# A rotation by 90 degrees: the first store held back until all loads but the last megabyte have landed

## The chip, the cores and the metric

The kernel runs on one core of a Trainium2 chip. The metric is device time in microseconds (us). Before the change the median of three runs is 123.41 us (123.36 to 123.59). Besides these runs there is one profiled execution, whose trace has the start and length of each instruction, each DMA packet and each semaphore update.

## The reference

The input is 32 x 3 images of 256 x 256 float32 (25.17 MB), and each is turned by a quarter:

```python
def setup_inputs():
    batch, c, h, w = 32, 3, 256, 256
    return {"x": np.random.randn(batch, c, h, w).astype(np.float32)}

def reference(x: np.ndarray) -> np.ndarray:
    return np.rot90(x, k=-1, axes=(-2, -1)).astype(np.float32)
```

Nothing is computed: every element is read once, moved, and written once, 50.33 MB in all.

## The kernel before, in words

All the data fits in SBUF at once. The rows of all images are cut into twelve slabs of 2 MB (128 partitions x 16 rows of 256 elements), which are held in five groups of 2, 2, 4, 2 and 2 slabs. A group is one tile (named u for each) with a buffer of its own, so no load ever waits for a buffer.

Loading. SP (SyncE) issues all loads from one queue. Group 0 comes in as two transfers of 1 MB (L55) and one of 2 MB (L56); groups 1 to 4 come in as ten transfers of 2 MB each (L61), two, four, two and two of them. A transfer of a group with I slabs fills every I-th partition, with both halves (index a) of each partition's row; in the last group it is 64 partitions x 2 halves x 16 KB. In all there are thirteen loads.

Turning. DVE transposes 32 x 32 blocks, a quarter of a group's data at a time, and writes the result in reversed order to where it belongs (L69 for group 0; L85 and L90 for the others). A quarter that would overwrite data still needed goes to a spare buffer first (L85, in PSUM or in one extra tile of SBUF), and ACT copies it home later (L75, L95). There are 24 DVE instructions of 3.6 to 4.0 us and 16 ACT copies of 0.5 to 1.9 us.

Storing. The same queue of SP issues twelve stores of 2 MB: two for group 0 (L103), ten for groups 1 to 4 (L108), in the order of the groups. In SP's program all stores stand behind all loads. The first store of each group waits for the group's last DVE instruction and ACT copy.

Two things set the order around the change. First, SP works its program through in order: an instruction that waits holds back everything behind it. Secondly, the framework gives the transfers of this queue eight semaphores in turn, and a transfer that reuses one waits until the transfer that had it before has landed; so at most eight transfers are open at a time. Before the change, the first store (L103) waits for the landing of load 5 (counted from 0) and for DVE and ACT, and is issued at 27.73 us; the second is issued at 32.51 us.

Of the kernel before, what the change touches and what calls it, by code (L numbers as in the profile page):

```python
# [1 line left out]

# [4 lines left out]


@with_exitstack  # L10
def kernel(
    ctx: ExitStack,
    tc: tile.TileContext,
    x: bass.AP,
    out: bass.AP,
):

    nc = tc.nc
    fp32 = mybir.dt.float32

    B, C, H, W = x.shape
    P = nc.NUM_PARTITIONS
    R = 16  # L30
    E = R * W
    hw = R // 2
    low, high = slice(0, hw), slice(hw, R)

    rows_in = x.rearrange("b c h w -> (b c h) w")
    rows_out = out.rearrange("b c h w -> (b c h) w")

    sizes = (2, 2, 4, 2, 2)
    first = [sum(sizes[:n]) for n in range(len(sizes))]
    groups = [  # L40
        ctx.enter_context(tc.tile_pool(name=f"group{n}", bufs=1)).tile([P, s, E], fp32, name=f"u{n}")
        for n, s in enumerate(sizes)
    ]
    psum = ctx.enter_context(tc.tile_pool(name="psum", bufs=1, space=bass.MemoryType.PSUM))
    spare = [psum.tile([P, E // 2], fp32, name=f"spare{h}") for h in range(2)]
    extra = ctx.enter_context(tc.tile_pool(name="extra", bufs=1)).tile([P, E // 2], fp32, name="extra")

    def rows_of(rows, n):
        return rows[first[n] * P * R : (first[n] + sizes[n]) * P * R]


    ld = rows_of(rows_in, 0).rearrange("(s i p r) w -> s i p (r w)", s=2, i=2, p=P)
    home = [groups[0][:, s].rearrange("p (i f) -> p i f", i=2) for s in range(2)]
    for i in range(2):
        nc.sync.dma_start(out=home[0][:, i], in_=ld[1, i])  # L55
    nc.sync.dma_start(out=home[1], in_=ld[0].transpose([1, 0, 2]))  # L56
    for n in range(1, len(sizes)):
        I = sizes[n]
        ld = rows_of(rows_in, n).rearrange("(a i m r) w -> i m a (r w)", a=2, i=I, m=P // I)
        for i in range(I):  # L60
            nc.sync.dma_start(  # L61
                out=groups[n].rearrange("p s f -> p (s f)").rearrange("p (a f) -> p a f", a=2)[i::I],
                in_=ld[i])

    def turn_slab(src, dsts):
        s = src.rearrange("p (i r g c) -> p c r g i", i=2, r=R // 2, c=R)
        for h, d in enumerate(dsts):
            d = d.rearrange("p (c k r) -> p c r k", c=hw, r=R // 2)[:, :, ::-1, ::-1]
            nc.vector.transpose(out=d, in_=s[:, h * hw : (h + 1) * hw])  # L69

    u = groups[0]
    turn_slab(u[:, 0], spare)
    turn_slab(u[:, 1], [u[:, 0, : E // 2], u[:, 0, E // 2 :]])
    for h in range(2):
        nc.scalar.copy(out=u[:, 1, h * E // 2 : (h + 1) * E // 2], in_=spare[h])  # L75

    def turn_group(n, held):
        I = sizes[n]
        T = I // 2
        K = W // (R * T)  # L80
        u = groups[n].rearrange("p s f -> p (s f)")
        src = u.rearrange("p (a t r g c) -> p t c r g a", a=2, t=T, r=R, c=R)
        dst = u.rearrange("p (i c k t r) -> p t c r k i", i=I, c=R, k=K, t=T)[:, ::-1, :, ::-1, ::-1, :]
        for t in range(T):
            nc.vector.transpose(  # L85
                out=held[t].rearrange("p (i c k r) -> p c r k i", i=I, c=hw, k=K)[:, :, ::-1, ::-1, :],
                in_=src[:, t, low, low])
        for c, r in ((low, high), (high, high), (high, low)):
            for t in range(T):
                nc.vector.transpose(out=dst[:, t, c, r], in_=src[:, t, c, r])  # L90
        back = u.rearrange("p (i c k t r) -> p t i c k r", i=I, c=R, k=K, t=T)[:, ::-1]
        for t in range(T):
            kept = held[t].rearrange("p (i c k r) -> p i c k r", i=I, c=hw, k=K)
            for i in range(I):
                nc.scalar.copy(out=back[:, t, i, low, :, high], in_=kept[:, i])  # L95

    for n, held in enumerate(([extra], spare, [spare[0]], [spare[1]]), 1):
        turn_group(n, held)


    st = rows_of(rows_out, 0).rearrange("(s i m r) w -> i m s (r w)", s=2, i=2, m=P // 2)
    for a in range(2):
        nc.sync.dma_start(out=st[a], in_=groups[0][a::2])  # L103
    for n in range(1, len(sizes)):
        st = rows_of(rows_out, n).rearrange("(a i m r) w -> a m i (r w)", a=2, i=sizes[n], m=P // 2)
        for i in range(0, sizes[n], 2):
            for a in range(2):
                nc.sync.dma_start(out=st[a][:, i : i + 2], in_=groups[n][a::2, i : i + 2])  # L108


# [1 line left out]
_INS = ['x']  # L112
_OUTS = [((32, 3, 256, 256), 'float32')]


# [23 lines left out]
```

## Time and profile before

| what | value |
|---|---|
| median of three runs | 123.41 us |
| profiled execution | 123.44 us |
| its span | 121.6 us |
| DVE busy | 87.4 us, 24 instructions |
| ACT busy | 14.9 us, 17 instructions |
| bytes moved | 50.33 MB, half read from HBM, half written |
| mean rate over the span | 414 GB/s |
| first issue of a load / of a store | 0.73 us / 27.73 us |
| last issue of a store | 104.56 us |

Times in the profile count from the start of the span; the profiled execution's own time is 1.84 us above its span. The profile gives the busy time of each engine, the mean share and rate of the sixteen DMA engines in forty equal slices of the span (3.04 us each), groups of instructions by source line, who waited for whom, and for a DMA issue the time from issue to landing. Landing means the update that completes the transfer's semaphore: each of the sixteen DMA engines adds one when its share is done. An issue row is written as start, length of the issue on SP's queue (SPq), line, and the tiles out<-in. In a stretch of time the columns are DVE, ACT and POOL busy time with their instruction counts, the granted clock of TensorE (not used here), the DMA share and GB/s.

### The profile page before, as it was taken

Reading aid. Unit: us, or ns where it says so; the run is one execution under the profiler, and the core shown is the slowest. Engines: PE = TensorE matmul, PEld = TensorE weight load, DVE = VectorE, ACT = ScalarE, POOL = GpSimd, SP = SyncE. Lnnn points to the kernel's source line nnn. Section 1 sums busy time; section 2 is a strip of 40 time slices with the busy share of each in tenths; the row PEclk is TensorE's granted clock in tenths of the full one; section 3 lists DMA queues with packets and bytes.
Section 4 is the critical chain, followed back from the end, with each engine's and each line's share of the span. In section 5 each row is a group of like instructions: output and inputs, shape, how many; then the busy total and the mean of one; then the engine's idle time right before and its main releaser. Section 6 shows DMA issues by size and latency. Waiting matters only on the chain.

```text
span 121.6 us, 130 instructions
## 1 busy us (share of the span) xinstructions
DVE 87.4 (72%) x24; ACT 14.9 (12%) x17; POOL 0.2 (0%) x4
## 2 busy tenths in 40 slices
DVE  0039999999994099999999949999999995000000
ACT  0000400470004100000000354000240004100000
POOL 0000000000000000000000000000000000000000
DMA  4999999998989899999999999999999999999993
GB/s 92 423 426 434 442 431 431 436 506 356 506 356 506 350 431 431 426 431 431 377 409 431 431 431 431 442 431 431 431 431 442 431 436 431 431 431 431 431 431 135
DMA packets 3472, 50.33 MB, mean 414 GB/s; under 512 B 400, under 2 KB 400, under 8 KB 400
## 3 DMA queue, kind: packets, MB, share of 16 engines
q1 hardware_dynamic: 3472, 50.33, 97.7%
HBM read 25.17 MB, written 25.17 MB: 414 GB/s over the span
## 4 chain that ended last, share of the span: by engine, by line
DVE 42%; DMA 30%; issue 7%; SPq 4%; ACT 2%; ACTq 1%; DVEq 0%
DVE u L90 30%; DMA u<-in_x_dram 30%; DVE spare L85 12%; SPq L61 3%; ACT u L95 2%; ACTq L134 1%; SPq L55 1%; SPq L56 0%; DVEq L85 0%
## 5 line engine op out<-in xcount | busy, mean ns | idle before, releaser
L90 DVE STREAM_TRANSPOSE u<-u 128x2048 f32<-128x2048 f32 x15 | 54.7, 3665 | 0.4
L85 DVE STREAM_TRANSPOSE spare<-u 128x2048 f32<-128x2048 f32 x4 | 14.3, 3586 | 5.9 <-DMA u<-in_x_dram 4.3
L95 ACT COPY u<-spare 128x512 f32<-128x512 f32 (+1 forms) x12 | 8.0, 743 | 55.9 <-DVE u L90 55.9
L69 DVE STREAM_TRANSPOSE spare<-u 128x2048 f32<-128x2048 f32 x2 | 7.1, 3584 | 8.1 <-DMA u<-in_x_dram 8.1
L69 DVE STREAM_TRANSPOSE u<-u 128x2048 f32<-128x2048 f32 x2 | 7.8, 3990 | 0.0
L75 ACT COPY u<-spare 128x2048 f32<-128x2048 f32 x2 | 3.6, 1870 | 8.7 <-DVE u L69 8.7
L85 DVE STREAM_TRANSPOSE extra<-u 128x2048 f32<-128x2048 f32 x1 | 3.9, 3899 | 0.0
L95 ACT COPY u<-extra 128x1024 f32<-128x1024 f32 x2 | 2.0, 1043 | 11.3 <-DVE u L90 11.3
L75 ACT ACT_TABLE_LOAD x1 | 1.3, 1283 | 13.1 <-DMA u<-in_x_dram 13.1
L123 POOL MEMSET const-bfloat16-1.0<- 128x1 bf16 x1 | 0.1, 101 | 0.0
L123 POOL MEMSET const-uint8-127<- 128x1 uint8 x1 | 0.1, 101 | 0.0
L123 POOL MEMSET const-float32-0.0<- 128x1 f32 x1 | 0.1, 98 | 0.2 <-issue 0.2
L123 POOL MEMSET const-float32-1.0<- 128x1 f32 x1 | 0.1, 98 | 0.0
## 6 DMA issues: line engine op xcount, KB each, us to landing
out_dram<-u SPq DMA_DIRECT2D x12, 2048.0 KB, 20.6
u<-in_x_dram SPq DMA_DIRECT2D x11, 2048.0 KB, 32.3
u<-in_x_dram SPq DMA_DIRECT2D x2, 1024.0 KB, 5.8
```

Source lines behind the costliest of these rows:

```text
L55: nc.sync.dma_start(out=home[0][:, i], in_=ld[1, i])
L61: nc.sync.dma_start(out=groups[n].rearrange("p s f -> p (s f)").rearrange("p (a f) -> p a f", a=2)[i::I], in_=ld[i])
L69: nc.vector.transpose(out=d, in_=s[:, h * hw : (h + 1) * hw])
L75: nc.scalar.copy(out=u[:, 1, h * E // 2 : (h + 1) * E // 2], in_=spare[h])
L85: nc.vector.transpose(out=held[t].rearrange("p (i c k r) -> p c r k i", i=I, c=hw, k=K)[:, :, ::-1, ::-1, :], in_=src[:, t, low, low])
L90: nc.vector.transpose(out=dst[:, t, c, r], in_=src[:, t, c, r])
L95: nc.scalar.copy(out=back[:, t, i, low, :, high], in_=kept[:, i])
L123: nc = _bacc.Bacc("TRN2", target_bir_lowering=False, num_devices=1)
L134: with _tile.TileContext(nc) as tc:
```

## The change

The last load, the second of group 4, is issued as two transfers of 1 MB: first half a = 0 of its 64 partitions, then half a = 1. The first of the two is called the mark. The first store of group 0 gets one more wait: it isn't issued before the mark has landed. As every other store stands behind it on SP, none of them is issued before that either. At that time all loads have landed but the second half of the last one, 1 MB. The number of transfers goes from 25 to 26; DVE and ACT have the same instructions in the same order.

```diff
     for n in range(1, len(sizes)):
         I = sizes[n]
         ld = rows_of(rows_in, n).rearrange("(a i m r) w -> i m a (r w)", a=2, i=I, m=P // I)
+        to = groups[n].rearrange("p s f -> p (s f)").rearrange("p (a f) -> p a f", a=2)
         for i in range(I):
-            nc.sync.dma_start(
-                out=groups[n].rearrange("p s f -> p (s f)").rearrange("p (a f) -> p a f", a=2)[i::I],
-                in_=ld[i])
+            if (n, i) == (len(sizes) - 1, I - 1):
+                mark = nc.sync.dma_start(out=to[i::I, 0], in_=ld[i][:, 0])
+                nc.sync.dma_start(out=to[i::I, 1], in_=ld[i][:, 1])
+            else:
+                nc.sync.dma_start(out=to[i::I], in_=ld[i])
...
     for a in range(2):
-        nc.sync.dma_start(out=st[a], in_=groups[0][a::2])
+        put = nc.sync.dma_start(out=st[a], in_=groups[0][a::2])
+        if a == 0:
+            tc.add_manual_dep(put.ins, mark.ins.name, mybir.DependencyInfo(
+                mybir.DependencyClass.Sync, mybir.DependencyReason.SCHED_ONLY), reason="stores after loads")
```

## The prediction

> **What bounds the kernel now.** I read the page's busy shares and the line of slices first, then the DMA queue, then stretches of time around the change from loading to storing, then single transfers from issue to landing, and last what SP (the queue that issues every transfer) waits for.
>
> From the page:
>
> ```profile
> span 121.6 us, 130 instructions
> DVE 87.4 (72%) x24; ACT 14.9 (12%) x17; POOL 0.2 (0%) x4
> DMA  4999999998989899999999999999999999999993
> GB/s 92 423 426 434 442 431 431 436 506 356 506 356 506 350 431 431 426 431 431 377 409 431 431 431 431 442 431 431 431 431 442 431 436 431 431 431 431 431 431 135
> q1 hardware_dynamic: 3472, 50.33, 97.7%
> ```
>
> DVE, the busiest engine, is idle for 28% of the span. The DMA engines are busy in every slice and 97.7% in sum: 50.33 MB at some 431 GB/s is 116.8 us of the 121.6. So bytes on one queue bound the kernel, and only a change of the rate, or a hole in the stream, can move the end. (The swings 506/356 come with the 32 KB packets of the third group: a packet is booked in the slice where it starts; their mean is 431.) The one lasting dip is in slices 20 and 21, 377 and 409.
>
> Stretches of time; the last two columns are the DMA engines' busy share and GB/s:
>
> ```profile
> 1.00:3.00 2.00, 0.00 (x0) 0.00 (x0) 0.00 (x0) 1.00 0.64 131
> 45.00:59.00 14.00, 13.93 (x5) 0.00 (x0) 0.00 (x0) 1.00 1.01 430
> 59.00:61.50 2.50, 2.50 (x2) 0.00 (x0) 0.00 (x0) 1.00 1.06 367
> 61.50:64.00 2.50, 2.47 (x2) 0.00 (x0) 0.00 (x0) 1.00 0.98 419
> 64.00:90.00 26.00, 24.27 (x7) 6.03 (x10) 0.00 (x0) 1.00 1.00 430
> 90.00:118.00 28.00, 11.83 (x4) 1.93 (x2) 0.00 (x0) 1.00 1.01 434
> ```
>
> Loads before 59 and stores after 64 run at the same 430 GB/s. Between them, with engines "busy" all the time, the rate is 367: packets take longer there. Now single transfers, issue row first, then its KB and us to landing: the last two loads and the first store.
>
> ```profile
> 17.90 0.60 SPq L61 DMA_DIRECT2D u<-in_x_dram  x1
> u<-in_x_dram SPq DMA_DIRECT2D x1, 2048.0 KB, 39.0
> 22.80 0.60 SPq L61 DMA_DIRECT2D u<-in_x_dram  x1
> u<-in_x_dram SPq DMA_DIRECT2D x1, 2048.0 KB, 39.6
> 27.73 0.65 SPq L103 DMA_DIRECT2D out_dram<-u  x1
> out_dram<-u SPq DMA_DIRECT2D x1, 2048.0 KB, 39.6
> DMA to landing us min/median/max: 4.8/5.8/6.9
> ```
>
> Landings are 17.90+39.0 = 56.9, 22.80+39.6 = 62.4, 27.73+39.6 = 67.3. So although the first store is issued at 27.7, it lands after the last load: the queue serves in the order of issue, and stores already run after loads. What the early issue does is to have the store stand directly behind the last load. The semaphore records give the landings finer: 52.00, 56.89 | 62.44 | 67.31, 72.17. The steps are 4.89 between loads, 5.55 for the last load, 4.87 and 4.86 for stores. So the last load, the only one with a store behind it, takes 0.66 us longer, and no step after it makes that up. Packet by packet, an engine's last two load packets (611 to 619 ns elsewhere) take some 700 and up to 1150 ns, from 59.0 on; all later store packets take 611. Eight of the sixteen engines come out of this 0.2 to 0.4 us late, eight about 0.75 us late, and these eight are last in every later transfer to the end. (The last row of the fence is the two 1 MB loads at the start: the first, issued at 0.73, lands 4.8 us later at 5.52, the second at 8.02.)
>
> SP's own waits, longest in total first:
>
> ```profile
> SPq L108 <- DVE u L90: 52.6, 4, 28.5
> SPq L134 <- DMA out_dram<-u: 14.7, 2, 14.5
> SPq L61 <- DMA u<-in_x_dram: 14.7, 4, 4.3
> SPq L108 <- ACT u L95: 8.9, 4, 3.0
> SPq L103 <- DMA u<-in_x_dram: 8.3, 2, 4.2
> ```
>
> L61 and L103 wait for landings: eight semaphores are used in turn, so at most eight transfers are open. L108 waits for the turned tiles.
>
> **The change part by part.** The sum is made against the profiled execution: 123.44 us (span 121.6), 0.03 above the median of the three runs, 123.41.
>
> *The last load in two.* One more issue of about 0.4 us on SP (the 1 MB issues at L55 take 0.37 and 0.42), in a stretch where SP only waits for landings: nothing, covered by 34 us of queued loads. Sixteen more completion packets, 9 ns each on its engine: 0.01 us. Both halves use 16 KB packets as before and spread over the same engines. Cost 0.0.
>
> *The turn of the semaphores.* One more transfer shifts it by one place: the stores of the first two groups wait for landings of loads 7 to 10 (at or before 52.0), all older than the mark. DVE waits for both halves of the last group's second load, but starts that group at 87.4. Cost 0.0.
>
> *The added wait on SP.* Queued behind it are all other stores, nothing else; DVE and ACT don't wait for stores. So group 2's stores are issued at 74.4 as before, set by DVE. The queue then holds four stores (groups 0 and 1) from 62 on, 4 x 4.87 = 19.5 us, to 81 or so; group 2's stores come 7 us before they are needed, the last group's (103.9) 7 us before the end of those ahead (111.1). The four held stores, issued back to back, need 0.6 + 3 x 1.25 = 4.4 us on SP (0.6 and 1.2 to 1.35 from the L108 issues at 74 to 79), less than one store's 4.87 us of streaming. Hence only the moment when the first store reaches the engines counts.
>
> *The handover.* (1) The mark, half of a 4.89 us load, lands at 56.89 + 2.45 = 59.34. (2) SP passes its wait and issues 0.08 later (the same event-and-issue pair took 27.66 to 27.73 here): 59.42. (3) From issue to landing on empty engines is known from one row: 4.8 us for 1 MB, of which 2.45 is streaming; 2.35 is start, first-byte latency and completion. A 2 MB store so started lands at 59.42 + 2.35 + 4.87 = 66.64. (4) A stream without any hole would give last load 56.89 + 4.89 = 61.78, first store 66.65. The two agree: the wait lands just in time, the last megabyte (2.45) hides what the late issue costs (0.08 + 2.35), with nothing to spare. (5) Against 67.31 now, that is -0.66 us: the stretched load packets go, if they come from store work taken up while loads are unfinished, since the stores now stand there only from about 60.4 (59.42 plus 1.0, from the first issue at 0.73 to the first packet at 1.74) instead of all along.
>
> Bounds. Below: -0.66, the whole loss gone. Above: nothing in this trace starts a store on an idle or draining queue, so its start-up is unknown; the nearest row is the load of (3), and the farthest reasonable case is that the whole 2.35 begins only when the last load has landed: 61.78 + 2.35 + 4.87 = 69.0, +1.7 us. I take a value near the lower end, since SP needs no landing of the last half: of the 0.66, I give back 0.2 to 0.25, because stores' completions are spread over 0.82 us (66.49 to 67.31) where loads' are over 0.43 (56.46 to 56.89), and half of this spread may belong to stores as such. Sum: -0.66 + 0.2 to 0.25 = -0.43, 123.44 - 0.43 = 123.0.
>
> A rule that speaks against this: the Trainium skill, DMA: Bandwidth & Descriptors, Rules for kernel authors, says to issue a DMA early and wait late, so that the fixed setup cost overlaps; the section on the anatomy of one DMA puts that cost at about 2.0 us for another issuing path. The start row here, 2.35, is near it. If the rule's cost lay fully bare, the time would be an estimated 123.44 - 0.66 + 2.0 = 124.8; the row with its 2.45 of cover makes it 123.0.
>
> **The rivals.** 0.2% is 0.25 us, about what a measurement of this kernel can tell from no change.
>
> *A: the 0.66 us belongs to turning from reading to writing HBM.* Then any order of issue pays it once. For it: all stores' landings keep the two sets of eight engines, to the end, and the loss is there with the engines full. Against: it is the load packets that stretch, not the first stores, and the sets are delayed unequally, which a fixed latency wouldn't do. Time 123.4 (123.2 to 123.65).
>
> *B: the first store comes too late, and the queue runs dry: slower.* For it: cover 2.45 against 2.43 needed is no margin, SP waits for the slowest of sixteen engines, and a store's first data may take longer than a load's. Against: the engines hold descriptors of the last half for 2.4 us while only SP's 0.08 and about 1.0 to the first packet have to pass. Break-even lies at a start-up of 2.35 + 0.66 = 3.0 us; above 3.26 it is measurably slower. At an excess of 1.1 us, between break-even and the far bound, 123.44 + 0.45 = 123.9.
>
> *C: the wait doesn't bind.* It does: without it SP issues at 27.7. No chance given.
>
> **How the numbers follow.** Clean handover 0.48 (123.0, own range 122.7 to 123.2); rival A 0.23 (123.4); rival B 0.29 (123.9, own range 123.65 to 125.1, most of it below 124.1). The likeliest gives the prediction. The range 122.65 to 124.0 reaches from the whole loss gone, with 0.1 for the spread of runs, over A, to two thirds of B; it leaves out a tenth at the top and little below. Faster 0.48, same 0.23, slower 0.29.
>
> **What would show it.** In the profile after: the first store's issue near 59.4; the slices around 60 at 420 or more where there were 377 and 409, and the last load's second half landing near 61.8, if step (5) holds; the first store landing near 66.7 to 66.9, and the following at 4.87 us each; group 2's first store still at 74.4. The same dip with stores landing at 67.3 would be A. A slice well under 350, and the first store landing after 67.6, would be B. The prediction fails if a store's start-up on draining engines isn't like a load's, or if the unequal delay of the engines comes back in whatever order the stores are issued.

## The result, and the profile after

The changed kernel takes 123.10 us (median of seven runs, 123.04 to 123.38) against 123.57 us of the kernel before on the same occasion (123.21 to 123.62): a ratio of 0.9972 with a 95% interval of 0.9959 to 0.9985. A second set of twelve runs on another chip gave 0.9982 (0.9965 to 0.9999); its medians are only 0.08 us apart, 123.19 against 123.27. So the kernel became faster by two or three tenths of a percent, where some 0.35% was forecast (-0.43 of 123.44 us). In all that follows, "before" is the kernel before on the same chip as the run beside it.

The page of the changed kernel, the lines that answer to those shown of before:

```profile
span 121.3 us, 134 instructions
DVE 87.2 (72%) x24; ACT 14.9 (12%) x17; POOL 0.2 (0%) x4
GB/s 92 427 421 438 454 432 432 438 497 357 508 357 508 351 421 432 427 432 421 432 432 427 421 432 432 432 421 416 416 427 432 432 432 432 432 432 432 432 432 173
q1 hardware_dynamic: 3488, 50.33, 97.6%
```

The dip is gone: slices 20 and 21 now have 432 and 432 GB/s, where they had 377 and 409. In the two stretches that the prediction read, the first rises from 367 to 406 GB/s, and the second stays at 419 (DMA share and GB/s in the last two columns):

```profile
59.00:61.50 2.50, 2.50 (x2) 0.00 (x0) 0.00 (x0) 1.00 0.96 406
61.50:64.00 2.50, 2.49 (x1) 0.00 (x0) 0.00 (x0) 1.00 0.99 419
```

The 406 falls short of the 430 of a full stream, in part because a packet is booked where it starts, and in part because for a moment near 60.9 up to three of the sixteen engines have no packet (0.2 us, summed over the engines). The landings below show what the whole passage costs. DVE and ACT are as they were. In exchange some later slices lie at 421 or 416 where there was 431; they matter below.

Single transfers of the changed kernel, issue row and then its KB and us to landing: the mark, the last half of the loads, the first store and the last store.

```profile
22.88 0.50 SPq L63 DMA_DIRECT2D u<-in_x_dram  x1
u<-in_x_dram SPq DMA_DIRECT2D x1, 1024.0 KB, 36.5
27.74 0.49 SPq L64 DMA_DIRECT2D u<-in_x_dram  x1
u<-in_x_dram SPq DMA_DIRECT2D x1, 1024.0 KB, 34.1
59.56 0.68 SPq L106 DMA_DIRECT2D out_dram<-u  x1
out_dram<-u SPq DMA_DIRECT2D x1, 2048.0 KB, 7.2
104.65 1.39 SPq L114 DMA_DIRECT2D out_dram<-u  x1
out_dram<-u SPq DMA_DIRECT2D x1, 2048.0 KB, 15.7
```

The mark lands at 59.4, the rest of the loads at 61.9, the first store at 66.75 and the last at 120.4. By the semaphore records: load 11 lands at 56.98, the last load at 61.87, the first store at 66.75, the last at 120.40. Before, it was 56.89, 62.44, 67.31 and 120.79. From load 11 to the first store it takes 9.77 us where it took 10.42: the handover, as this passage is called here, is 0.65 us shorter. From the first store to the last it takes 53.65 us where it took 53.48: 0.17 us is given back. The rest is that all loads landed 0.09 us later in this execution. Together -0.65 + 0.17 + 0.09 = -0.39 at the last landing, and -0.34 in the two profiled executions, 123.44 and 123.10.

What SP waited for, in the changed kernel:

```profile
SPq L106 <- DMA u<-in_x_dram: 31.2, 1, 31.2
SPq L114 <- DVE u L93: 26.2, 3, 10.4
SPq L140 <- DMA out_dram<-u: 14.2, 1, 14.2
SPq L114 <- ACT u L98: 6.9, 3, 3.0
```

SP now stands 31.2 us in one wait at the first store, and that costs nothing by itself: the queue had loads all the time. The stores of group 2 are still issued at 74.5, on DVE's word.

### The profile page after: what moved, and what is told of

It reads as the page before. It is cut to its first block, busy times and chain, and to the rows that moved or that the text cites. A ratio compares the mean times of both kernels' runs of the same rounds, so it can differ in the third digit from the quotient of the medians.

```text
span 121.3 us, 134 instructions
## 1 busy us (share of the span) xinstructions
DVE 87.2 (72%) x24; ACT 14.9 (12%) x17; POOL 0.2 (0%) x4
## 4 chain that ended last, share of the span: by engine, by line
DVE 42%; DMA 30%; issue 7%; SPq 4%; ACT 2%; ACTq 1%; DVEq 0%
DVE u L93 30%; DMA u<-in_x_dram 30%; DVE spare L88 12%; SPq L66 3%; ACT u L98 2%; ACTq L140 1%; SPq L55 1%; SPq L56 0%; DVEq L88 0%
```

## The experiments

Three theories stood against each other at first. Theory 1 is that of the prediction: load packets stretch because store work stands right behind them. Theory 2: the split itself helps. Theory 3: any held store helps, whenever it comes.

### The split alone

The last load is split as in the change, and no store waits for the mark:

```diff
         put = nc.sync.dma_start(out=st[a], in_=groups[0][a::2])
-        if a == 0:
-            tc.add_manual_dep(put.ins, mark.ins.name, mybir.DependencyInfo(
...
```

> The last load goes in two transfers; no store waits for the mark. Theory 1 (load packets stretch because store work stands directly behind them in the queue while loads are unfinished): the stores stand there as before, so the last load's second half lands some 5.5 us after load 11, the rate around 60 us is 370 again, and the time is that of the kernel before, within 0.1 us. Theory 2 (the split itself, smaller last transfers with the half a = 0 first, removes the stretch): the last load takes 4.9 us, and the time is 0.4 us below before.

Measured: 123.45 us, ratio 0.9996 (0.9985 to 1.0008). Stretches around the handover:

```profile
59.00:61.50 2.50, 2.50 (x2) 0.00 (x0) 0.00 (x0) 1.00 1.06 374
61.50:64.00 2.50, 2.50 (x1) 0.00 (x0) 0.00 (x0) 1.00 0.98 419
```

The dip is back, 374 GB/s. The last megabyte lands at 62.34, 2.77 us after the one before it (59.57) instead of 2.45. Theory 2 falls: the split by itself is worth nothing that these runs can tell. The wait is what counts. The expected step of some 5.5 us from load 11 (57.13) was 5.21, so the stretch was only half as large in this execution.

### Two megabytes left

No split; the wait is for the last load but one:

```diff
-            if (n, i) == (len(sizes) - 1, I - 1):
-                mark = nc.sync.dma_start(out=to[i::I, 0], in_=ld[i][:, 0])
...
+            got = nc.sync.dma_start(out=to[i::I], in_=ld[i])
+            if (n, i) == (len(sizes) - 1, 0):
+                mark = got
```

> No split; the first store waits for the last load but one, so 2 MB are left when it is issued. Theory 1: issue at 57.0, first store work at the engines from 58.0 (1.0 us later), before the stretch began (59.0), so the stretch is there in full: the last load takes 5.5 us, the time is that of before within 0.1 us. Theory 3 (any held store helps, since few transfers are then open or since SP issues them late): the last load takes 4.9 us, 0.4 us below before.

Measured: 123.33 us, ratio 0.9990 (0.9980 to 1.0001), between the two expectations.

```profile
59.00:61.50 2.50, 2.50 (x2) 0.00 (x0) 0.00 (x0) 1.00 0.97 387
```

The dip is there, about half as deep: the last load takes 62.03 - 56.89 = 5.14 us, 0.25 more than a load does. The stores were issued from 57.03 on; with the 1.33 us from issue to first packet that the run with nothing left shows below, they stood at the engines at an estimated 58.4, before the load packets began to stretch (from 59.25 here). That a held store can still come with a dip speaks against theory 3. That the stretch isn't there in full speaks against theory 1 in its plainest form, but weakly: the profiled execution, 123.00 us, is the fastest of the twelve, and the others may have had more of it.

### Half a megabyte left, on half the partitions

```diff
-                mark = nc.sync.dma_start(out=to[i::I, 0], in_=ld[i][:, 0])
-                nc.sync.dma_start(out=to[i::I, 1], in_=ld[i][:, 1])
+                nc.sync.dma_start(out=to[i::I, 0], in_=ld[i][:, 0])
+                mark = nc.sync.dma_start(out=to[i::I, 1][:32], in_=ld[i][:32, 1])
+                nc.sync.dma_start(out=to[i::I, 1][32:], in_=ld[i][32:, 1])
```

> The last load in 1 + 0.5 + 0.5 MB, the first store waits for the second of these, so 0.5 MB are left, 1.2 us of streaming. Mark at 60.7, issue at 60.8. By the start row of the loads (2.35 us of start and completion beside streaming) the first store lands at 60.8 + 2.35 + 4.87 = 68.0, 1.25 us later than with 1 MB left (66.75): time 0.85 us above before. If a store starts faster than a load, less: with 1.0 us to the first packet and no more, the queue has stores at 61.8, about when the loads end (61.4 to 61.9), and the time is that of the changed kernel, 0.4 below before, to 0.2 above before.

Measured: 126.10 us, ratio 1.0217 (1.0198 to 1.0235), far beyond both. The stretches show why:

```profile
45.00:58.00 13.00, 12.93 (x5) 0.00 (x0) 0.00 (x0) 1.00 1.01 430
60.00:63.00 3.00, 3.00 (x2) 0.00 (x0) 0.00 (x0) 1.00 0.88 191
```

The two half-megabyte loads, one into partitions 1 to 63 and one into 65 to 127, run at about half rate: packets of 16 KB take some 1.2 us instead of 0.61, and the two land 2.25 and 2.26 us after what came before them (62.37 and 64.63) instead of 1.2. So this run says nothing of the cover of half a megabyte at full rate (the cover is the time for which loads still in the queue keep the engines at work after the first store's issue). That is measured below with every second partition.

### Nothing left

All stores wait for the second half of the last load.

```diff
-                mark = nc.sync.dma_start(out=to[i::I, 0], in_=ld[i][:, 0])
-                nc.sync.dma_start(out=to[i::I, 1], in_=ld[i][:, 1])
+                nc.sync.dma_start(out=to[i::I, 0], in_=ld[i][:, 0])
+                mark = nc.sync.dma_start(out=to[i::I, 1], in_=ld[i][:, 1])
...
+    def put(**k):
+        p = nc.sync.dma_start(**k)
+        tc.add_manual_dep(p.ins, mark.ins.name, mybir.DependencyInfo(
...
```

> All stores wait for the last load (its second half): no cover at all. Last landing 61.9, issue 62.0. By the start row of the loads the first store lands at 62.0 + 2.35 + 4.87 = 69.2, 2.45 us later than in the changed kernel, so the time is 2.0 us above before. With 1.0 us to the first packet, 4.87 of streaming and 0.35 to the landing it is 68.2: 1.0 us above before. This measures a store's start on an empty queue, which decided between the likeliest case and the slower rival.

Measured: 125.57 us, ratio 1.0173 (1.0159 to 1.0188), 2.03 us above before. The first store, and the hole in the stream (DMA share and GB/s in the last two columns):

```profile
62.06 0.68 SPq L105 DMA_DIRECT2D out_dram<-u  x1
out_dram<-u SPq DMA_DIRECT2D x1, 2048.0 KB, 6.9
61.00:63.00 2.00, 2.00 (x1) 0.00 (x0) 0.00 (x0) 1.00 0.00 0
```

This is the row that the prediction lacked, a store on an empty queue. Its first packet starts 1.33 us after the issue (62.06 to 63.40; the first load of the kernel took 1.0), and it lands 6.87 us after the issue, 2.0 beyond its streaming, where the load's row gave 2.35. From load 11 (57.04) to the first store (68.93) it is 11.89 us, against 9.76 for a stream without a hole: the hole costs 2.13 us.

### Half a megabyte left, over all partitions

```diff
-                mark = nc.sync.dma_start(out=to[i::I, 0], in_=ld[i][:, 0])
-                nc.sync.dma_start(out=to[i::I, 1], in_=ld[i][:, 1])
+                nc.sync.dma_start(out=to[i::I, 0], in_=ld[i][:, 0])
+                mark = nc.sync.dma_start(out=to[i::I][0::2, 1], in_=ld[i][0::2, 1])
+                nc.sync.dma_start(out=to[i::I][1::2, 1], in_=ld[i][1::2, 1])
```

> As the run before with 0.5 MB left, but each half-megabyte transfer takes every second partition of its set, over all 128 partitions, where the earlier one took partitions 1 to 63 only and ran at half the rate. If that half rate was due to the narrow set of partitions, all transfers now stream at 430 GB/s. Then the mark lands at 60.6, the issue is at 60.8, and with the store's start measured with nothing left (62.06 to 68.93, that is 6.87 us to landing, 2.0 beyond streaming) the first store lands at 67.65, 0.9 us later than with 1 MB left: time 0.4 to 0.7 us above before. If the half rate was due to the small size, it stays at 215 GB/s and the time is 2.5 us above before again.

Measured: 124.43 us, ratio 1.0084 (1.0063 to 1.0104), 1.1 us above before. The half-megabyte loads now land 1.22 us apart (59.35, 60.57, 61.79), which is full rate, so the small size wasn't the reason for the half rate. What differs is the set of partitions, and with it which rows of HBM each half reads; no run separates these two. The Trainium skill has a ground for the partitions (DMA: Bandwidth & Descriptors, The descriptor swizzle): in a transfer over all partitions it assigns partitions 0 to 63 to the eight even ports and 64 to 127 to the eight odd ones. By that map 32 partitions out of 1 to 63 leave half of the ports idle, and the trace agrees: 191 GB/s in the stretch from 60 to 63 us, and some 230 by the landings 2.26 us apart, against 430.

```profile
60.71 0.68 SPq L107 DMA_DIRECT2D out_dram<-u  x1
out_dram<-u SPq DMA_DIRECT2D x1, 2048.0 KB, 7.0
59.00:61.50 2.50, 2.50 (x2) 0.00 (x0) 0.00 (x0) 1.00 0.74 315
61.50:64.00 2.50, 2.47 (x2) 0.00 (x0) 0.00 (x0) 1.00 0.90 374
```

The store is at the engines at 62.04, 1.33 us after its issue again, while the last load's packets end at 61.3; the first store lands 10.76 us after load 11, 1.0 more than without a hole. So what must be covered is 2.1 to 2.2 us: 0 + 2.13 with nothing left, 1.22 + 1.0 with half a megabyte left. One megabyte covers 2.45. The first store landed where it was expected (67.67 against 67.65); the time lies above the 0.4 to 0.7 us expected, since the stores after it ran slower too, 53.87 us from first to last where the kernel before takes 53.48.

### One and a half megabytes left

```diff
-                mark = nc.sync.dma_start(out=to[i::I, 0], in_=ld[i][:, 0])
+                mark = nc.sync.dma_start(out=to[i::I][0::2, 0], in_=ld[i][0::2, 0])
+                nc.sync.dma_start(out=to[i::I][1::2, 0], in_=ld[i][1::2, 0])
                 nc.sync.dma_start(out=to[i::I, 1], in_=ld[i][:, 1])
```

> Mark of 0.5 MB (every second partition), so 1.5 MB are left: it lands at 58.1, issue at 58.3, store work at the engines from 59.4 to 59.6. Theory 1, with engines that take up queued work 2.2 us ahead (from 59.0 for loads that end at 61.3): a part of the stretch, 0.1 to 0.3 us, comes back; time 0.2 to 0.4 us below before, between 2 MB left and 1 MB left. Theory 3 (any held store helps alike): as with 1 MB left.

Measured: 122.93 us (122.86 to 123.02), ratio 0.9968 (0.9957 to 0.9978).

```profile
GB/s 84 430 433 419 452 433 433 433 519 346 519 346 519 346 433 427 427 433 411 411 417 427 433 427 433 433 433 433 433 427 433 433 433 433 433 433 433 433 433 173
59.00:61.50 2.50, 2.50 (x2) 0.00 (x0) 0.00 (x0) 1.00 0.98 419
104.56 1.40 SPq L115 DMA_DIRECT2D out_dram<-u  x1
out_dram<-u SPq DMA_DIRECT2D x1, 2048.0 KB, 15.6
```

No part of the stretch came back, against the expectation. (The slices at 411 and 417 are a matter of where a packet is booked: load packets there take 611 to 617 ns, and the last load lands 4.89 us after load 11.) The first store lands 9.84 us after load 11, the last 53.41 us after the first: neither the stretch nor what the changed kernel gave back. Theory 3 falls here, if narrowly: this interval and that of two megabytes left (0.9980 to 1.0001) don't overlap, so it matters when the held store comes.

### A copy between the loads and the stores

What is it in a store that stretches the loads: that the engine reads SBUF, or that it writes HBM? The kernel before, with a copy of SBUF to SBUF behind the last load:

```diff
+    nc.sync.dma_start(out=groups[0][0::2], in_=groups[0][0::2])
     for a in range(2):
         nc.sync.dma_start(out=st[a], in_=groups[0][a::2])
```

> The kernel before with one more transfer of 2 MB directly behind the last load: half of group 0's finished tile is copied onto itself, SBUF to SBUF, which leaves the data as it is. It adds its own streaming, 4.87 us if reading and writing SBUF go side by side, 9.8 if they share a rate. If the load packets stretch because the engines read SBUF ahead for what follows, the last load still takes 5.2 to 5.55 us, and the first store behind the copy shows no further loss. If they stretch because of the coming writes to HBM, the last load takes 4.9 us and the loss of 0.3 to 0.66 shows where the stores follow the copy.

Measured: 128.17 us (one run). The transfers: last load, copy, first store.

```profile
22.75 0.60 SPq L61 DMA_DIRECT2D u<-in_x_dram  x1
u<-in_x_dram SPq DMA_DIRECT2D x1, 2048.0 KB, 39.5
27.67 0.53 SPq L102 DMA_DIRECT2D u<-u  x1
u<-u SPq DMA_DIRECT2D x1, 2048.0 KB, 39.4
32.45 0.65 SPq L104 DMA_DIRECT2D out_dram<-u  x1
out_dram<-u SPq DMA_DIRECT2D x1, 2048.0 KB, 39.5
```

The landings are 62.26, 67.09 and 71.97, and load 11's is 56.83. The last load takes 5.43 us, 0.54 too long, though the transfer right behind it only reads and writes SBUF; the copy takes 4.83 and the store after it 4.88, so the passage from the copy to writing HBM costs nothing. In this one run, then, no write to HBM is needed for the stretch. What the copy and a store have in common is that they read SBUF, and that they don't read HBM; which of the two it is, and how it slows the load packets, isn't shown.

### Stores between loads

Group 0's two stores issued ahead of the last group's loads:

```diff
-    for n in range(1, len(sizes)):
+    def load(n):
...
+    for n in range(1, len(sizes) - 1):
+        load(n)
...
+    st = rows_of(rows_out, 0).rearrange("(s i m r) w -> i m s (r w)", s=2, i=2, m=P // 2)
+    for a in range(2):
+        nc.sync.dma_start(out=st[a], in_=groups[0][a::2])
+    load(len(sizes) - 1)
...
```

> The kernel before with group 0's two stores issued ahead of the last group's two loads, so the queue turns three times (loads, stores, loads, stores). Theory 1: every turn from loads to stores stretches the loads' tail by 0.25 to 0.66 us, so the second such turn adds that; the turn back to loads costs between nothing and as much again: time 0.25 to 1.3 us above before. Rival: the stretch belongs to the end of loading, not to a turn: within 0.1 us of before.

Measured: 123.73 us (123.41 to 124.12), ratio 1.0026 (1.0011 to 1.0041), on the low edge of theory 1. The two passages from loads to stores in the profile:

```profile
49.00:51.50 2.50, 2.47 (x2) 0.00 (x0) 0.00 (x0) 1.00 0.91 282
70.00:72.50 2.50, 1.31 (x1) 1.16 (x3) 0.00 (x0) 1.00 1.00 426
```

At the first, the last load ahead of the stores takes 52.65 - 47.11 = 5.54 us, a full stretch; at the second, 72.20 - 67.31 = 4.89, none. The profiled execution (123.42 us) is one of the fastest of this kernel, and the extra time of the others isn't seen in it. So a turn can cost some 0.65 us or nothing, and the sum over turns can't be foretold by counting them.

### The changed kernel and the version with 1.5 MB left, on one chip

Theory 4, formed on the runs above: with 1 MB left, the stores come just too late for some engines, and what was given back after the handover follows from that.

> The changed kernel again, beside the version with 1.5 MB left, on one chip. Theory 4 (with 1 MB left some engines just run dry at the handover, and stores that began so take 617 ns a packet instead of 611): last load without a stretch, store packets of 614 to 618 ns, landings 4.88 us apart, time 0.2 to 0.4 us below before.

> The version with 1.5 MB left again. Theory 4: no stretch and no dry engine, store packets of 611 ns, landings 4.86 us apart, so 0.15 to 0.2 us below the changed kernel on the same chip, 0.4 to 0.55 below before. Rival: the two are the same within 0.1 us, and the earlier difference was that of two chips.

A third kernel has the finer split but the later mark, so 1 MB is left:

```diff
-                mark = nc.sync.dma_start(out=to[i::I][0::2, 0], in_=ld[i][0::2, 0])
-                nc.sync.dma_start(out=to[i::I][1::2, 0], in_=ld[i][1::2, 0])
+                nc.sync.dma_start(out=to[i::I][0::2, 0], in_=ld[i][0::2, 0])
+                mark = nc.sync.dma_start(out=to[i::I][1::2, 0], in_=ld[i][1::2, 0])
```

> The last load split as in the version with 1.5 MB left (0.5 + 0.5 + 1 MB, every second partition), but the store waits for the second half-megabyte, so 1 MB is left as in the changed kernel. Theory 4 (what is left counts): as the changed kernel, store packets of 614 to 618 ns, 0.15 to 0.2 us above the version with 1.5 MB left. Rival (the finer split is what helps): as the version with 1.5 MB left, 611 ns.

And the kernel before, once more:

> The kernel before, a second profile, to see how far the stretch differs from one execution to another: last load's step 5.2 to 5.6 us, store packets of 611 ns, within 0.2 us of before.

| kernel | median, us | ratio to before (95%) | mean store packet, ns | mean step of store landings, us |
|---|---|---|---|---|
| 1 MB left, the changed kernel | 123.19 (123.08 to 123.31) | 0.9982 (0.9965 to 0.9999) | 615.7 | 4.877 |
| 1 MB left, finer split | 123.24 (123.11 to 123.45) | 0.9987 (0.9970 to 1.0004) | 614.7 | 4.879 |
| 1.5 MB left | 122.96 (122.85 to 123.16) | 0.9961 (0.9945 to 0.9978) | 611.1 | 4.869 |
| before | 123.27 (123.01 to 124.01) | | 611.1 | 4.862 |

(Packets of 16 KB that start between 70 and 115 us in the profiled execution; the step is the time from the first store's landing to the last, over 11.) The version with 1.5 MB left is 0.23 us below the changed kernel on the same chip, and this order was expected. Against the kernel before, both gain less than was expected: 0.08 and 0.31 us by the medians, where 0.2 to 0.4 and 0.4 to 0.55 stood. In the two profiles (123.28 and 123.16 us) the handover is the same, 9.77 and 9.79 us, and 0.09 of the 0.12 us between them come after the first store. The split isn't the reason, since with it and 1 MB left the time is that of the changed kernel. What is left when the stores are issued counts, and 1.5 MB is better than 1 MB, 2 MB and 0.5 MB. This version beats both kernels. (That it beats 2 MB and 0.5 MB is read from ratios on different chips.)

The second profile of the kernel before:

```profile
59.00:61.50 2.50, 2.50 (x2) 0.00 (x0) 0.00 (x0) 1.00 1.00 367
```

Its last load took 5.36 us, a stretch of 0.47 where the first profile had 0.66. These two profiles differ by 0.19 us in the stretch and by 0.20 in time (123.44 and 123.24). So the stretch varies, and the time with it as far as two executions show. The times of the kernel before spread over 1.0 us here (29 runs), those of the kernels without a stretch over 0.23 and 0.31 (12 runs each); that all of this spread is the stretch isn't shown.

Theory 4's first half isn't shown. Stores that come 1.33 us after their issue reach the engines of the changed kernel at 60.9, and the first engines end their loads at 60.8, so it is a close thing; but the time in which an engine has no packet there, summed over the engines, is 0.2 and 0.0 us in its two profiles (0.0 in both with 1.5 MB left), less than the 1.1 and 1.3 us that the kernel before has in its dip, and that kernel's stores ran at 611 ns nevertheless.

## Why the prediction was right, point by point

*The number.* Forecast was 123.0 us, 0.43 below the profiled execution before; 123.10 came out, 0.34 below in the profiles and 0.47 by the medians of the first set, but 0.08 by those of the second. That the number came so near is in part luck: the kernel before alone spreads over 1.0 us, and one term of the sum, below, was right for a wrong reason.

*The bound and the covers.* DMA bytes set the end, DVE's and ACT's work and the second half of SP's program didn't move, and split, semaphore turn and extra issue cost nothing: the split alone measured 0.9996. An issue of 1 MB took 0.49 to 0.50 us where 0.4 was put, under cover; the four held stores were issued in 4.2 us where 4.4 was put. One reading was off by a place without harm: the stores of the first two groups reuse the semaphores of loads 6 to 9, not 7 to 10; the last of these landed at 47.19.

*Steps (1) and (2).* The mark landed at 59.42, where 59.34 was forecast; all loads were 0.09 us later in that execution. The issue followed 0.14 us later, not 0.08; one more wait stands before it, which may be why.

*Step (3), the start of a store.* Taken from the first load as 2.35 us, it is 2.0 on an empty queue. This was mis-sized by 0.35 us, on the safe side: cover 2.45 against a need of 2.1 to 2.2, where the prediction saw no margin at all.

*Steps (4) and (5).* From load 11 to the first store 9.76 us was forecast and 9.77 came out; the whole stretch went, 0.65 of 0.66. The mechanism of step (5), store work taken up while loads are unfinished, is supported by the held stores and by the copy run: loads stretch before a transfer that only reads and writes SBUF. The stretched packets were read a little short: one of them took 1265 ns, not up to 1150. But the condition isn't as simple as put there. Stores that reach the engines at an estimated 58.4 (issue plus 1.33; 2 MB left) gave a stretch of 0.25 us, those at 59.6 (1.5 MB left) none, and one of two passages in the run with stores between loads had none with the stores long in the queue.

*The 0.2 to 0.25 us given back.* The size was near, and the reason was wrong. It was argued from the wider spread of store landings, as a delay of the first store. In fact the first store had none (4.88 us after the last load, 0.01 more than without a hole); the stores after it ran at 615.9 ns a packet on average instead of 611, and their landings, 4.877 us apart instead of 4.862, lose 11 x 0.015 = 0.17 us in all. So the term was about right in size by luck.

*Rival A*, a fee for turning from reading to writing HBM, falls: no loss at the turn in the changed kernel, and none from copy to stores. *Rival B*, stores too late, is real, but begins below 1 MB: with 0.5 MB left the kernel is 0.84% slower, with nothing left 1.73%. The 0.23 us by which 1 MB left is behind 1.5 MB may be a mild form of it, which isn't shown.

*The rule.* The Trainium skill (DMA: Bandwidth & Descriptors, Rules for kernel authors) says to issue early so that the setup overlaps, and the section on the anatomy of one DMA gives about 2.0 us of fixed cost for another issuing path. The size agrees with the 2.0 to 2.13 us measured here. The rule holds as far as the cover goes: issuing the first store some 32 us later, at 59.56 instead of 27.73, cost nothing while 1 MB of loads was left, and 2.03 us in all with none.

## What to carry to other kernels

When a queue of transfers bounds the kernel, look for the place where it passes from loads to stores: stores right behind loads, or a copy out of SBUF, made the last load land 0.25 to 0.66 us later here, with the DMA share still at 0.97 to 1.06, so it shows in GB/s and in landings, not in the busy share. Holding the first store back until what is left exceeds its start with a margin (here the start is 2.1 to 2.2 us, and 1.5 MB, 3.7 us of loads, did best) takes this away, and made the times steadier here; cover that is too short costs more than the stretch, 1.1 us with half a megabyte left and 2.0 with nothing. When a transfer is split by partitions, taking every second one kept the full rate here, and the lower and the upper half didn't.

## What was not expected of the hardware

From the handover to the end, stores ran at 611.0 to 611.1 ns a packet on average in the profiles of the kernel before, of the split alone, with 2 and 1.5 MB left, with the copy, and with stores between loads; and at 614.7 to 616.9 ns with 1 MB left, with half a megabyte left and with nothing left. That is 0.17 to 0.5 us over eleven steps (4.877 to 4.907 us against 4.862 in the kernel before). The slow ones are those in which stores arrive late, but why that should last for 50 us stays open: neither the time without a packet nor how far the sixteen engines' landings of the first store are apart (0.51 us in the changed kernel, 0.49 with 2 MB left) sorts the cases. At the last store they are sorted: the engines are 0.18 to 0.26 us apart in the slow profiles and 0.39 to 0.83 in the others; whether that is cause or effect isn't shown.

In its one run, the copy of SBUF to SBUF moved its 2 MB in 4.83 us, the time of a load or a store of that size, although it reads and writes SBUF at once.
